# Streaming two tiles through two layers instead of one tile through both, in an eight-core hybrid decoder step

## The chip, the cores and the metric

The kernel runs on all eight NeuronCores of one Trainium2 chip. Each core has its own data and no core talks to another. The metric is the device time of one execution in microseconds (us), taken from the slowest core. The program has a second, slower state in which one die runs at a lower granted clock (in one run of the kernel before: 731.43 us, with 0.756 to 0.768 on cores 0 to 3 and 0.853 to 0.856 on the others); runs in that state are left out of every comparison.

Engines are named as in the profile: PE is TensorE's matmul, PEld its weight load, DVE is VectorE, ACT is ScalarE, POOL is GpSimd, SP is the queue that issues loads and stores. The program gives each engine one queue of instructions and orders the engines against each other by semaphores. A wait therefore also holds back what stands behind it in the same queue; the timelines below show this, GpSimd's above all (on ACT, in e8, a square that waited 11.15 us).

## The reference, cut to what matters

Per core there is one prompt sequence of 2048 tokens and 16 sample sequences of 4 tokens. Both go through two layers and a final norm:

```
def recurrent_layer(x, ...):                      # layer 0
    u = rmsnorm(x, g)
    xb, gate = split(u @ w_in)                    # 1024 -> 2 x 1024
    xc = causal_conv(xb)                          # 4 taps
    r, i = sigmoid(block-diagonal gates of xc)    # 8 blocks of 128
    a = exp(-8 r softplus(-lam));  h_t = a h_{t-1} + sqrt(1 - a^2) i xc
    return x + (h * silu(gate)) @ w_out

def pool_layer(x, ...):                           # layer 1
    u = rmsnorm(x, g)
    xb, gate = split(u @ w_in)
    z = ((windowed mean of xb over 2, 4, 8, 16) - xb) @ w_grp ...
    return x + (z * silu(gate)) @ w_out
y = rmsnorm(pool_layer(recurrent_layer(x)), final_norm)
```

The recurrence, the convolution and the pooling carry state from one tile of 512 tokens to the next, so the four prompt tiles of a layer must stay in order. Layer 1 of a tile and layer 0 of the next tile are independent of each other.

## The kernel before

A helper records each operation with what it reads and writes, derives the semaphore waits, and emits one in-order queue per engine. A layer of a tile is cut into four steps of two 128-channel chunks. The parts:

```
# The norm of one 128-token row group s of a tile; XS and the PSUM banks PS0/PS1 exist twice, UT once.
def N2(tl, s, key):   # POOL: XS[s % 2] = X * rstd
    S.run("pool", tensor_scalar(out=xs, in0=X, scalar1=ssc, ...), reads=[bXB[b][s], bSS], writes=[bXS[s % 2]])
def N3(tl, s):        # PE: eight 128x128 transposes into bank s % 2
    S.run("pe", trf, reads=[bXS[s % 2], bIDB], writes=[bPS[tb]])
def N4(tl, s, grow):  # DVE: UT[:, :, rows of s] = bank * gain
    S.run("dve", tensor_tensor(out=UT[:, :, s*128:...], in0=tbv, in1=gbc, op=mult), reads=[bPS[tb], bVT], writes=[bUTs[s]])

def inproj(l, tl, m, psi):   # PE: eight matmuls over all four row groups of UT
    S.run("pe", f, reads=bUTs + [bW_in[l][widx]], writes=[bPS[psi]])

def A1evac(l, tl, j):        # per chunk: the halo on POOL, the chunk on DVE (layer 0) or ACT (layer 1)
    S.run("pool", tensor_copy(out=ext[:, 0:HL], in_=Hh[:, c, :]), writes=[bEXT[ci]])
    S.run("dve" or "act", copy(out=ext[:, HL:HL+Tt], in_=PS[2 + 2*ci]), writes=[bEXT[ci]])
    S.run("pool", tensor_copy(out=Hh[:, c, :], in_=ext[:, Tt:Tt+HL]), reads=[bEXT[ci]])
# ... E0b: multiply, scan and gate on DVE, and on POOL a copy of the scan's last column into HSTp

def layer0(tl, next_tl):
    ...
    for j in range(4):
        if j + 1 <= 3: A1evac(0, tl, j + 1)
        if j == 3:     out_part1(0, tl)
        E0a(tl, j)
        if j + 1 <= 3: A1silu(0, tl, j + 1); CASTRI(tl, j + 1)
        E0b(tl, j)
        if j + 1 <= 3: TANHV(tl, j + 1)
        if j + 2 <= 3: A1pe(0, tl, j + 2)      # the projection runs one step ahead
# then out_part2 per row group, residual add, square, N2, N3, N4, and layer1 of the same tile
```

Inside a layer the input projection of step j+2 is queued at the end of step j, so PE runs a step ahead. At the end of a layer everything drains: output projection, residual add, norm, and only then the next layer's first projection.

## Time and profile before

The median is 705.5 us (five runs, 703.8 to 706.41).

| what | us | from |
|---|---|---|
| first projection of the first tile | 31.15 | timeline of PE |
| one tile in the steady state, two layers and two seams | 147.2 | timeline of PE |
| sample projection starts | 623.97 | timeline of PE |
| end of the span | 702.3 | page |
| PE, DVE, ACT, POOL busy | 488, 457, 343, 144 | page |
| granted clock, mean | 0.85 to 0.86 | cores |

Two groups of the kernel before, from the page's list of costliest instructions. The columns are line, engine, operation, names and shapes, count, busy us and mean ns, then the idle time before them and the releaser of most of it:

```profile
L494 PE MATMUL PS<-UT,W_in 128*128 128x512 bf16 x1024 | 264.0, 423 | 10.5 <-DVE UT L472 10.5
...
L462 PE MATMUL PS<-IDENTB,XSreg 128*128 128x128 bf16 (+1 forms) x272 | 22.0, 228 | 34.0 <-POOL XSreg L450 14.0
```

The first is the input projection; PE hardly waits for its operand (10.5 us in all). The second are the transposes of the norms. PE was idle 34.0 us before them, of which 14.0 us ended with GpSimd's scaled row.

### The profile page before, as it was taken

How to read it: one execution, taken by the hardware profiler on the slowest of the kernel's cores; microseconds unless marked ns; L12 is line 12 of the kernel's file. 1: busy time of each engine (PE TensorE's matmuls, PEld its weight loads, DVE VectorE, ACT ScalarE, POOL GpSimd, SP SyncE). 2: the span in 40 equal slices, each digit the busy share in tenths (PEclk: the TensorE clock that was granted, in tenths of full speed). 3: DMA queues.
4: the chain of work that ended last, by engine and by line, in shares of the span. 5: the costliest groups of instructions: out<-in, count | busy, mean ns of one | idle time of the engine just before them, and what ended most of it. 6: DMA issues, size and time to landing. Idle time of an engine off the chain costs nothing.

```text
span 702.3 us, 8514 instructions; the slowest of 8 cores (700.1 to 702.3 us)
## 1 busy us (share of the span) xinstructions
PE 487.8 (69%) x2352; PEld 216.9 (31%) x2352; DVE 456.8 (65%) x670; ACT 343.4 (49%) x554; POOL 144.0 (21%) x270
## 2 busy tenths in 40 slices
PE   0476576898766687976766679786566889761645
PEld 0232223443322233433222234333222334341332
DVE  0668877583668866856588767746788668457262
ACT  1368863243078753533488735531778626324211
POOL 4213312120301113323011132412021223121000
PEclk9998978799998778999888789999876989996766
DMA  9999980300000000050000000420000001203003
GB/s 217 157 163 166 162 129 12 121 1 0 1 1 0 1 0 1 31 179 31 0 1 0 0 1 1 151 91 0 0 1 0 1 0 43 93 2 119 16 11 67
DMA packets 19845, 34.65 MB, mean 49 GB/s; under 512 B 3539, under 2 KB 12755, under 8 KB 19798
## 3 DMA queue, kind: packets, MB, share of 16 engines
q0 software_dynamic: 13552, 13.63, 13.8%
q1 hardware_dynamic: 6246, 20.46, 9.6%
q8 instruction: 20, 0.33, 0.2%
q14 instruction: 27, 0.22, 0.1%
HBM read 37.75 MB, written 9.97 MB: 68 GB/s over the span
## 4 chain that ended last, share of the span: by engine, by line
PE 41%; DVE 29%; issue 12%; ACT 12%; POOL 3%; DMA 2%; DVEq 1%; ACTq 0%; POOLq 0%; SPq 0%
PE PS L494 20%; PE PS L515 10%; DVE TMP L620 8%; DVE EXT L593 3%; PE PS L532 3%; DVE UT L472 3%; DVE H L682 3%; ACT JUNK L419 3%; DVE TMP L616 3%; DMA XSreg<-vecs 2%; PE PS L755 2%; DVE TMP L679 2%; ACT A2M L764 2%; PE PS L893 1%; POOL XSreg L450 1%
## 5 line engine op out<-in xcount | busy, mean ns | idle before, releaser
L494 PE MATMUL PS<-UT,W_in 128*128 128x512 bf16 x1024 | 264.0, 423 | 10.5 <-DVE UT L472 10.5
L494 PEld LDWEIGHTS PS<-UT,W_in 128*128 128x128 bf16 x1024 | 109.8, 108 | 162.7 <-issue 67.6
L515 PE MATMUL PS<-W_out,HG 128*128 128x512 bf16 x288 | 73.5, 420 | 13.5 <-ACT TMP L608 9.0
L620 DVE SCALAR_TENSOR_TENSOR TMP<-EXT,VT,TMP 128x512 f32<-128x512 f32 x96 | 72.1, 751 | 10.7 <-DVE TMP L620 0.5
L638 PE MATMUL PS<-XCB,W_r 128*128 128x512 bf16 x32 | 15.8, 495 | 81.9 <-ACT XCB L628 43.4
L532 PE MATMUL PS<-W_out,HG 128*128 128x512 bf16 (+1 forms) x256 | 62.1, 403 | 9.7 <-DVE HG L773 9.1
L608 ACT ACTIVATE TMP<-PS 128x512 f32<-128x512 f32 x64 | 35.8, 598 | 60.5 <-PE PS L494 60.4
L538 DVE TENSOR_TENSOR XB<-PS,XB 128x512 f32<-128x512 f32 (+1 forms) x68 | 44.8, 687 | 29.8 <-PE PS L532 26.0
L596 ACT ACTIVATE EXT<-PS 128x512 f32<-128x512 f32 x32 | 19.1, 598 | 84.4 <-PE PS L494 55.1
L450 POOL TENSOR_SCALAR XSreg<-XB,SS 128x1024 bf16<-128x1024 f32 (+1 forms) x34 | 37.9, 1118 | 64.6 <-ACT SS L423 43.0
L515 PEld LDWEIGHTS PS<-W_out,HG 128*128 128x128 bf16 x288 | 30.0, 106 | 58.5 <-issue 32.3
L472 DVE TENSOR_TENSOR UT<-PS,VT 128x1024 bf16<-128x1024 bf16 (+1 forms) x34 | 39.3, 1187 | 10.3 <-PE PS L462 10.3
L462 PE MATMUL PS<-IDENTB,XSreg 128*128 128x128 bf16 (+1 forms) x272 | 22.0, 228 | 34.0 <-POOL XSreg L450 14.0
L773 DVE TENSOR_TENSOR HG<-A2M,TMP 128x512 bf16<-128x512 f32 x32 | 21.2, 688 | 37.6 <-ACT A2M L764 37.6
L695 POOL COPY HSTp<-H 128x1 f32<-128x1 f32 x32 | 22.2, 694 | 107.8 <-DVE H L682 107.8
L682 DVE TENSOR_TENSOR_SCAN H<-TR,HSTp,TMP 128x512 f32<-128x512 f32 x32 | 41.1, 1284 | 3.8 <-DVE TMP L679 1.0
L641 ACT ACTIVATE TR<-PS,DER 128x512 f32<-128x512 f32 x32 | 21.9, 685 | 38.0 <-DVE H L682 32.0
L532 PEld LDWEIGHTS PS<-W_out,HG 128*128 128x128 bf16 (+1 forms) x256 | 26.3, 105 | 45.3 <-issue 20.4
L764 ACT ACTIVATE A2M<-PS,DER,VT 128x512 f32<-128x512 f32 x32 | 23.1, 776 | 35.0 <-PE PS L755 35.0
L593 DVE COPY EXT<-PS 128x512 f32<-128x512 f32 x32 | 22.0, 687 | 27.9 <-PE PS L494 27.9
L729 DVE TENSOR_TENSOR TMP<-TMP 128x512 f32<-128x512 f32 (+3 forms) x48 | 33.5, 697 | 5.4 <-DVE TMP L729 0.5
L419 ACT ACTIVATE JUNK<-XB 128x1024 uint8<-128x1024 f32 (+1 forms) x21 | 21.9, 1045 | 27.8 <-DVE XB L538 27.6
(142 smaller groups left out, 640.8 us busy)
## 6 DMA issues: line engine op xcount, KB each, us to landing
y_p<-XB SPq DMA_DIRECT2D x16, 512.0 KB, 3.5
XB<-x_p SPq DMA_DIRECT2D x12, 512.0 KB, 4.8
W_in<-a_w_in POOLq DMA_DIRECT2D x4, 1024.0 KB, 28.3
W_in<-b_w_in POOLq DMA_DIRECT2D x4, 1024.0 KB, 20.9
XB<-x_p SPq DMA_DIRECT2D x1, 2048.0 KB, 11.6
W_out<-a_w_out POOLq DMA_DIRECT2D x2, 1024.0 KB, 49.1
W_out<-b_w_out POOLq DMA_DIRECT2D x2, 1024.0 KB, 23.4
XB<-st_pool SPq DMA_DIRECT2D x15, 64.0 KB, 5.6
```

Of the source, the lines that this page charges most:

```text
L419: S.run("act", lambda e: e.activation(out=junk, in_=X, func=AF.Square, accum_out=ssc), reads=[bXB[b][s]], writes=[bJUNK, bSS])
L450: S.run(N2_ENG, lambda e: e.tensor_scalar(out=xs, in0=X, scalar1=ssc, scalar2=0.0, op0=ALU.mult, op1=ALU.add), reads=[bXB[b][s], bSS], wri ...
L472: S.run("dve", lambda e: e.tensor_tensor(out=UT[:, :, s * 128:s * 128 + np_], in0=tbv, in1=gbc, op=ALU.mult), reads=[bPS[tb], bVT], writes ...
L494: last = e.matmul(PS[psi][:, 0:Tt], lhsT=W_in[l][:, k, m * 128:(m + 1) * 128], rhs=UT[:, k, 0:Tt], start=(k == 0), stop=(k == NCH - 1))
L515: last = e.matmul(PS[psi][0:np_, :], lhsT=HG[:, k, s * 128:s * 128 + np_], rhs=W_out[l][:, k, half * 512:(half + 1) * 512], start=(i_ == 0 ...
L532: last = e.matmul(PS[psi][0:np_, :], lhsT=HG[:, k, s * 128:s * 128 + np_], rhs=W_out[l][:, k, half * 512:(half + 1) * 512], start=(i_ == 0 ...
L538: S.run("dve", lambda e, Xh=Xh, psi=psi: e.tensor_tensor(out=Xh, in0=PS[psi][0:np_, :], in1=Xh, op=ALU.add), reads=[bPS[psi], bXB[b][s]], ...
L593: S.run("dve", lambda e, ext=ext, ci=ci: e.tensor_copy(out=ext[:, HL:HL + Tt], in_=PS[2 + 2 * ci][:, 0:Tt]), reads=[bPS[2 + 2 * ci]], writ ...
L608: S.run("act", lambda e, q=q, ci=ci: e.activation(out=SG[q][:, 0:Tt], in_=PS[3 + 2 * ci][:, 0:Tt], func=AF.Silu), reads=[bPS[3 + 2 * ci]], ...
L620: S.run("dve", lambda e, k=k: e.scalar_tensor_tensor(out=xc, in0=ext[:, k * St:k * St + Tt], scalar=vcol(c, V_CW0 + k), in1=xc, op0=ALU.mu ...
L682: S.run("dve", lambda e, h=h, a=a, bt=bt, c=c: e.tensor_tensor_scan(out=h, data0=a, data1=bt, initial=HST[:, c, 0:1], op0=ALU.mult, op1=AL ...
L764: S.run("act", lambda e, mi=mi, c=c, zt=zt: e.activation(out=zt, in_=PS[6 + mi][:, 0:Tt], func=AF.Identity, scale=vcol(c, V_BSCALE), bias= ...
```

## The change

The intent is to fill the seams. The four tiles no longer go through both layers one by one. Eight stages (layer 0 of tiles 0 and 1, layer 1 of tiles 0 and 1, the same for tiles 2 and 3) form one stream of 32 steps. Two neighbouring stages are independent, so the output projection of a stage is issued in eight groups inside the following stage, and the norm of the stage to come is placed in the third step (p == 2) of the stage before it. HG, the operand of the output projection, is doubled for this; the pool state lies in the second copy and is loaded at the end. UT, the operand of the input projection, still exists once. The core of the diff:

```diff
-        HG = sb("HG", [128, NCH, T], BF16)
+        HGt = [sb("HG0", [128, NCH, T], BF16), sb("HG1", [128, NCH, T], BF16)]
...
-        PTW = [TMP[:, 2048 + i * EXTW:2048 + (i + 1) * EXTW] for i in range(2)]
+        PTW = [TMP[:, 3072:3072 + EXTW], XSreg[:, 0:EXTW]]
...
+        stages = [(0, tiles[0]), (0, tiles[1]), (1, tiles[0]), (1, tiles[1]),
+                  (0, tiles[2]), (0, tiles[3]), (1, tiles[2]), (1, tiles[3])]
...
+            for i in range(nt):
+                X, p, j = tasks[i]
...
+                norm = p == 2 and ln is not None
+                soon = norm and (ln == 1 or X == 0)
+                late = norm and not soon
...
+                rows = carry + add_pend()            # residual adds of the stage before
+                if soon:
+                    N2r(tn, 0, (lk, 0))
+                    N2r(tn, 1, (lk, 1))
+                back_a(i)
+                if l == 1:
+                    issue(X - 1, nc_)                # output groups of the stage before
+                if soon:
+                    N3(tn, 0)
+                    N3(tn, 1)
...
+                back_b(i)                            # scans; HSTp copies on POOL
...
+                if soon:
+                    N4(tn, 0, gr)
+                    N4(tn, 1, gr)
+                    N2r(tn, 2, (lk, 2))
+                    N2r(tn, 3, (lk, 3))
...
+                if norm:
+                    N3(tn, 2)
+                    N3(tn, 3)
+                    N4(tn, 2, gr)
+                    N4(tn, 3, gr)
...
+                if n2 is not None:
+                    front1(n2)                       # input projection, a step ahead
+                    issue(X if p == 3 else X - 1, 2)
```

N2r is the reciprocal root (two small POOL operations) and N2. "Late" are the two handovers at which the next tile must first be loaded over rows that are still being stored: out of stage X3 (layer 1 of tile 1) and out of stage X4 (layer 0 of tile 2). I call the change from one stage to the next a handover; there are seven, numbered by the stage X0 to X6 that they end.

## The prediction

> **What bounds the kernel now.** I read four views in this order: the slices of the page, the table of windows cut at the edges of one tile (185.4 us, when the second tile's first layer-0 projection starts, to 332.6 us, when the third tile's does), the timeline of VectorE inside one layer-0 step, and the timeline of TensorE across a layer's end. First the page:
>
> ```profile
> PE   0476576898766687976766679786566889761645
> DVE  0668877583668866856588767746788668457262
> PEclk9998978799998778999888789999876989996766
> ```
>
> Neither row is full: PE dips where DVE is high and the other way round, four times, once per tile. So no engine bounds the whole; two different ones bound two kinds of stretch. The windows say which (columns: stretch, length, busy of PE, PEld, DVE, ACT, POOL, granted clock, DMA share, GB/s):
>
> ```profile
> 216.36:232.32 15.96, 10.44 (x37) 3.94 (x36) 13.34 (x19) 12.67 (x19) 2.72 (x7) 0.82 0.01 1
> 248.70:272.09 23.39, 18.80 (x97) 8.62 (x98) 16.46 (x20) 13.19 (x26) 6.04 (x7) 0.86 0.00 1
> 286.00:293.80 7.80, 7.80 (x38) 3.56 (x37) 6.37 (x9) 4.77 (x9) 2.25 (x5) 1.00 0.01 2
> 309.14:332.63 23.49, 17.42 (x100) 8.34 (x101) 12.17 (x16) 5.94 (x10) 5.77 (x7) 0.99 0.23 68
> ```
>
> Row one is one of the four steps (two 128-channel chunks) of layer 0: DVE is busy 13.3 of 16.0 us. Row three is one of the four steps of layer 1: PE is busy all of it. Rows two and four are the seams, output projection plus residual add plus norm, after layer 0 and after layer 1: 23.4 and 23.5 us in which the next layer may not start. One tile is 63.3 us of layer 0 (185.40 to 248.70), a seam, 37.1 us of layer 1, a seam: 147.2 us.
>
> How full is DVE really in a layer-0 step? Its timeline:
>
> ```profile
> 229.20 0.69 DVE L697 TENSOR_TENSOR HG<-H,TMP 128x512 bf16<-128x512 f32 x1
> 229.81 0.68 DVE L679 TENSOR_TENSOR TMP<-TMP,A2M 128x512 f32<-128x512 f32 x1
> 230.60 1.28 DVE L682 TENSOR_TENSOR_SCAN H<-TR,HSTp,TMP 128x512 f32<-128x512 f32 x1
> ...
> 235.30 0.69 DVE L593 COPY EXT<-PS 128x512 f32<-128x512 f32 x1 [1.21 <-PE PS L494]
> 236.77 2.48 DVE L620 SCALAR_TENSOR_TENSOR TMP<-EXT,VT,TMP 128x512 f32<-128x512 f32 x3
> ```
>
> Between dependent instructions lies about 0.1 us that is not called idle; the only bracketed wait in the step is 1.21 us for PE. So a layer-0 step is 16.0 - 1.2 = 14.8 us of DVE work that nothing but DVE can shorten. The seam on PE:
>
> ```profile
> 247.05 0.63 PE L639 MATMUL PS<-XCB,W_i 128*128 128x512 bf16 x1
> 248.79 10.33 PE L515 MATMUL PS<-W_out,HG 128*128 128x512 bf16 x36 [1.11 <-DVE HG L697]
> 259.27 6.20 PE L532 MATMUL PS<-W_out,HG 128*128 128x512 bf16 x28
> 265.31 0.61 PE L462 MATMUL PS<-IDENTB,XSreg 128*128 128x128 bf16 x8
> ...
> 272.09 13.21 PE L494 MATMUL PS<-UT,W_in 128*128 128x512 bf16 x48 [1.48 <-DVE UT L472]
> ```
>
> 16.5 us of projection during which DVE finishes early and waits, then 6.8 us of square, scale, transpose, scale, then the next projection. 36 matmuls in 10.33 us is 287 ns each, 28 in 6.20 us is 221 ns: the first run partly at the low clock.
>
> [...] in layer 0 a run of matmuls starts 427 ns apart after the 3 to 4 us gaps around the gate matmuls and ends at 216 ns. [...] this trace shows clock 1.00 with PE full from 286 to 294 us on its core[...]. [...] the residual add measures 688. [...] The change leaves the number of loads in a layer-0 step at two.
>
> **The change part by part.** No arithmetic is taken away. Eight stages (layer 0 of tiles 0 and 1, layer 1 of tiles 0 and 1, the same for 2 and 3) make 32 steps in one stream. Two neighbouring stages are always independent, so the output projection of a stage (8 groups of 8 matmuls, over two PSUM banks), its residual adds, and the norm of the next but one are put among the steps of the following stage. HG is doubled for it, by laying the pool state over its second copy; so the pool state is loaded and transposed at the end instead of near the start.
>
> *Taken off:* the seams, 23.4 + 23.5 us a tile.
>
> *Put into a layer-0 stage*, on DVE, which bounds it: 8 adds at about 0.70 us spacing (7 took 4.87) = 5.6; 4 scalings into UT at about 1.15 = 4.6. Per stage: 4 x 14.8 = 59.2 + 10.2 = 69.4. At the third step all four UT pieces must be written before the next stage's projection may start, and DVE then waits for the first 8 of its matmuls, at 216 to 427 ns, 1.7 to 3.4 us, with the semaphores about 4. Total 73. A stage followed by layer 1 has no convolution in its last step: two scans with their multiplies 5.4 plus the widest pool 7.7, not 14.8, and PE is the next to wait on: 72. The stage after tile 1's layer 1 also gets 4 final scalings at 1.22 (4.9): 79. The first one has the small state transposes: 73. PE has room: its 16 gate, 128 input and 64 output matmuls and 32 transposes are 208 x 0.22 + 2.4 = 48 us at full clock, and filling its gaps should keep that clock.
>
> *A layer-1 stage* is bound by PE: (128 + 16 + 64) x 0.22 + 4 x 0.61 = 48 us. DVE has about 40: 20 tree adds and 8 subtractions over both chunks (19.5), 8 gates (5.5), 5.6, 4.6, up to 4.9. The norm chain (last add, square 1.25, rstd 0.5 to 1.4, scale 1.12, transpose 0.61, scaling 1.2, some 6 to 7 us) is entered in the third step with no projection left to cover it, so I add 5 to 6: 54, and 57 where the next is layer 0. The last stage has fewer projections and no next norm: 45.
>
> *Sum.* Start of the first projection 31 (measured 31.15), its first step 14.5 (45.73), stages 73 + 72 + 54 + 57 + 79 + 72 + 54 + 45 = 506, the last projection with the pool state's transposes mixed in 12: 564. In the old trace the sample tile's input projection begins at 623.97, and the rest to 702.3 is 78.3 us that the change reorders but hardly shortens. 564 + 78.3 = 642, plus the 3 us by which the time exceeds the span: **645 us**. Of the four tiles' 8 seams (188 us) I thus expect about 60 back; the other 128 us are the same matmuls, adds and scalings, put where DVE or PE is already the bound, and the new bubbles.
>
> **The rivals.**
> 1. *Full overlap.* Waits that I added as bubbles are covered (DVE's 4 us, PE's 5 to 6): stages of 69 and 49, about 38 us less, near 607; half of it 625. For it: PE's 4 us gaps and its cold start are just what is filled. Against: UT exists once, so each stage's first projection still hangs on four scalings.
> 2. *In-order stalls.* PE executes in order; an output group waits for DVE's add to free one of two banks, and the gate matmuls that feed ScalarE stand behind it. If each of the 16 layer-0 steps loses 2 us by that, +32: 677. Against: each add stands in DVE's order before the next group is needed.
> 3. *The clock falls.* [...] The trace before has dense stretches of 40 us without it.
> 4. *Loads at the start.* Tile 1's 2 MB is wanted by 78 us, while the weights fill the DMA engines to about 100 us (slices 1 to 6); ScalarE could stand 5 to 15 us in front of a square. Loading the pool state later gives 1 MB back.
>
> **Range and chances.** Rivals 2 and 4 in part and rival 1 in part give 622 to 670. Between 691 and 720 needs two rivals in full, or a stall that I don't see: 0.05; slower than 720: 0.02; faster than 691: 0.93.
>
> **What would show each step.** Right: the sample projection starts near 564 us; DVE over 85% busy in layer-0 stages; no stretch of 16 us with output matmuls alone; a recorded mean of the input projection's matmuls clearly below the old 423 ns, since the clock stays up; DVE's wait of about 4 us once per stage at the evacuation. DVE's total busy time near the old 457 us and PE's below 488, because only its cold share shrinks. Wrong: long waits of PE on bank-freeing adds (rival 2)[...], squares that wait for tile 1's load (rival 4), or a tail longer than 78 us. The prediction as a whole is wrong if the streamed stages are no shorter than 147 us a tile.

Where the recorded text is marked as cut, it gave rules and figures of the hardware that no trace or run of this case shows. No term of the sum went with them: it still reads 564 + 78.3 + 3, about 645 us. What is gone from rival 3 is its bill for a lower clock, which stood above the range of 622 to 670 us. The trace of the kernel before shows:

- After PE's wait of 2.10 us at 214.75 us (only two gate matmuls lie between) the projection starts with weight loads 427 ns apart and the granted clock is 0.50 from 215.55 to 218.95 us; from 220.65 us it is 1.00. Dense weight loads at 1.00 are 216 ns apart (253.78 to 258.63 us). This is what "cold" and "restart" mean below. That filled gaps keep the clock up was an expectation, which e3 tests; what "about 4" adds for semaphores is an estimate too (brackets of 0.17 and 0.23 us stand in the traces here).
- From 280 to 320 us PE is busy 34.1 of 40 us at a granted clock of 1.00: the "dense stretches" of rival 3.
- The mean residual add is 688 ns. The "loads in a layer-0 step" are ScalarE's table loads, 1283 ns each, for instance at 217.35 and 224.48 us.

## The result, and the profile after

The changed kernel takes 696.0 us (median of 9 runs, 695.13 to 700.07) against 705.3 us. A ratio is the mean time of one kernel's runs over that of the other's of the same rounds, so it isn't quite the ratio of the medians: here 0.988, with a 95 % interval of 0.986 to 0.989. The gain is real but within 2 %. The outputs are correct.

The page's slices of the kernel after (40 equal slices of the span, busy tenths; PEclk is the granted clock in tenths):

```profile
PE   0485666688389859936797167873898699761645
DVE  0657776888857655754688758898656567667262
PEclk9986766899689979976899659995999799985766
```

The dips of PE have not gone. They have become shorter and deeper: in the middle of the span single slices fall to 3, 3, 1 and 3, where the kernel before has none below 5, with drops of the granted clock (to 7, 6 or 5) next to them. The mean clock is 0.83 to 0.84, lower than before.

The windows of four stages after, cut at the first input projection of each stage (stretch, length, busy us of PE, PEld, DVE, ACT, POOL with counts, granted clock, DMA share, GB/s):

```profile
112.55:191.10 78.55, 56.66 (x240) 24.17 (x241) 64.49 (x84) 48.90 (x72) 19.65 (x38) 0.83 0.00 1
191.10:251.88 60.78, 49.00 (x236) 22.72 (x237) 40.37 (x68) 25.40 (x40) 15.45 (x30) 0.92 0.00 1
251.88:320.76 68.88, 51.16 (x240) 23.82 (x241) 39.68 (x52) 22.97 (x40) 19.25 (x36) 0.85 0.19 62
320.76:408.35 87.59, 58.05 (x244) 24.70 (x245) 64.28 (x84) 59.54 (x89) 21.54 (x42) 0.79 0.15 49
```

Stage X1 (layer 0) keeps DVE busy 64.5 of 78.6 us, stage X2 (layer 1) keeps PE busy 49.0 of 60.8. In both some 12 to 14 us belong to no bounding engine. X3 and X4, the late handovers, are worse. X1 to X4 carry two tiles in 295.8 us (112.55 to 408.35), 147.9 us a tile. The tile took 147.2 before. **The steady state has gained nothing**; the 8.6 us (sample projection at 615.42 instead of 623.97) come from the two ends of the stream.

The same two groups of the page as before, now after:

```profile
L502 PE MATMUL PS<-UT,W_in 128*128 128x512 bf16 x1024 | 256.4, 414 | 18.4 <-DVE UT L480 12.4
...
L470 PE MATMUL PS<-IDENTB,XSreg 128*128 128x128 bf16 (+1 forms) x272 | 30.4, 284 | 76.6 <-POOL XSreg L458 38.8
```

The projection's mean has gone from 423 to 414 ns only. PE's idle time before transposes has gone from 34.0 to 76.6 us, and the part released by GpSimd's rows from 14.0 to 38.8.

Here is one early handover, out of stage X1, on three engines. First PE's timeline (start, length, engine, line, operation, count, in brackets the idle time before it and the releaser):

```profile
176.24 0.61 PE L470 MATMUL PS<-IDENTB,XSreg 128*128 128x128 bf16 x8 [2.44 <-POOL SS L905]
177.99 1.01 PE L470 MATMUL PS<-IDENTB,XSreg 128*128 128x128 bf16 x8 [1.15 <-POOL XSreg L458]
...
181.91 0.63 PE L647 MATMUL PS<-XCB,W_i 128*128 128x512 bf16 x1
185.61 1.01 PE L470 MATMUL PS<-IDENTB,XSreg 128*128 128x128 bf16 x8 [3.07 <-POOL XSreg L458]
188.51 1.01 PE L470 MATMUL PS<-IDENTB,XSreg 128*128 128x128 bf16 x8 [1.88 <-POOL EXT L598]
191.10 9.24 PE L502 MATMUL PS<-UT,W_in 128*128 128x512 bf16 x34 [1.58 <-DVE UT L480]
```

Between 182.5 and 191.1 us PE does two us of transposes. It waits for GpSimd's rows, and then restarts on a low clock: 34 matmuls in 9.24 us are 272 ns each, at a granted clock of 0.50 from 191.10 to 194.50 us and 0.97 from there to 197.00. (The bracket at 188.51 names the halo copy of L598, because that ended last before it. By the code the transpose reads only the row, which ended at 188.26, 0.25 us before it, as at 185.61.) GpSimd in the same stretch:

```profile
182.33 0.71 POOL L707 COPY HSTp<-H 128x1 f32<-128x1 f32 x1 [2.08 <-DVE H L694]
183.12 0.19 POOL L903 TENSOR_SCALAR SS<-SS 128x1 f32<-128x1 f32 x1
183.46 0.55 POOL L905 TENSOR_TENSOR SS<-SS,NEGH 128x1 f32<-128x1 f32 x1
184.24 1.12 POOL L458 TENSOR_SCALAR XSreg<-XB,SS 128x1024 bf16<-128x1024 f32 x1 [0.23 <-POOL SS L905]
...
187.14 1.12 POOL L458 TENSOR_SCALAR XSreg<-XB,SS 128x1024 bf16<-128x1024 f32 x1 [0.23 <-POOL SS L905]
188.20 0.20 POOL L598 COPY EXT<-H1p 128x15 f32<-128x15 f32 x1
```

It copies the scan's last column (HSTp) only once DVE's scan has run; rows 2 and 3 stand behind that copy, and the halo copy of the next step stands behind the rows. DVE:

```profile
186.74 1.22 DVE L480 TENSOR_TENSOR UT<-PS,VT 128x1024 bf16<-128x1024 bf16 x1 [0.23 <-PE PS L470]
189.63 1.23 DVE L480 TENSOR_TENSOR UT<-PS,VT 128x1024 bf16<-128x1024 bf16 x1 [1.67 <-PE PS L470]
195.59 0.71 DVE L742 TENSOR_TENSOR TMP<-EXT 128x526 f32<-128x526 f32 x1 [4.74 <-ACT EXT L604]
```

DVE scales the last two row groups as they come, then has nothing until the projection's first output has been evacuated: 4.74 us. A late handover, out of stage X3, again on PE:

```profile
308.14 1.01 PE L470 MATMUL PS<-IDENTB,XSreg 128*128 128x128 bf16 x8 [9.13 <-POOL XSreg L458]
...
318.17 1.01 PE L470 MATMUL PS<-IDENTB,XSreg 128*128 128x128 bf16 x8 [4.08 <-POOL EXT L598]
```

The first transpose waits 9.13 us for its row and the last one 4.08 us more (for the row before the copy that the bracket names, as above). Here the reload takes part: ScalarE's squares at 309.18 and 314.18 us had waited 3.75 and 3.85 us for the load of tile 2.

### The profile page after: what moved, and what is told of

It is laid out like the page before. It is cut to its first block, busy times and chain, and to the rows that moved or that the text cites. A ratio compares the mean times of both kernels' runs of the same rounds, so it can differ in the third digit from the quotient of the medians.

```text
span 694.0 us, 8450 instructions; the slowest of 8 cores (690.7 to 694.0 us)
## 1 busy us (share of the span) xinstructions
PE 473.6 (68%) x2352; PEld 219.2 (32%) x2352; DVE 460.7 (66%) x670; ACT 336.4 (48%) x522; POOL 167.8 (24%) x320
## 4 chain that ended last, share of the span: by engine, by line
PE 43%; DVE 23%; issue 12%; ACT 12%; POOL 6%; DMA 3%; DVEq 1%; POOLq 0%; ACTq 0%; SPq 0%
PE PS L502 23%; PE PS L876 10%; DVE TMP L628 4%; DVE H L694 4%; POOL XSreg L458 3%; DVE TMP L691 2%; PE PS L943 2%; DVE UT L480 2%; DMA XSreg<-vecs 2%; DVE EXT L601 2%; POOL SS L905 2%; PE PS L540 2%; PE PS L768 1%; DVE TMP L624 1%; PE PS L470 1%
## 5 line engine op out<-in xcount | busy, mean ns | idle before, releaser
L502 PE MATMUL PS<-UT,W_in 128*128 128x512 bf16 x1024 | 256.4, 414 | 18.4 <-DVE UT L480 12.4
L502 PEld LDWEIGHTS PS<-UT,W_in 128*128 128x128 bf16 x1024 | 107.0, 105 | 164.1 <-issue 64.1
L876 PE MATMUL PS<-W_out,HG 128*128 128x512 bf16 x448 | 103.6, 383 | 4.2 <-DVE XB L885 4.2
L470 PE MATMUL PS<-IDENTB,XSreg 128*128 128x128 bf16 (+1 forms) x272 | 30.4, 284 | 76.6 <-POOL XSreg L458 38.8
L628 DVE SCALAR_TENSOR_TENSOR TMP<-EXT,VT,TMP 128x512 f32<-128x512 f32 x96 | 74.3, 774 | 10.7 <-DVE TMP L628 0.5
L885 DVE TENSOR_TENSOR XB<-PS,XB 128x512 f32<-128x512 f32 x64 | 43.9, 688 | 43.2 <-PE PS L876 38.7
L876 PEld LDWEIGHTS PS<-W_out,HG 128*128 128x128 bf16 x448 | 44.0, 98 | 58.3 <-issue 6.3
L777 ACT ACTIVATE A2M<-PS,DER,VT 128x512 f32<-128x512 f32 x32 | 23.1, 773 | 69.8 <-PE PS L768 69.8
L480 DVE TENSOR_TENSOR UT<-PS,VT 128x1024 bf16<-128x1024 bf16 (+1 forms) x34 | 39.8, 1188 | 24.5 <-PE PS L470 24.4
L895 ACT ACTIVATE JUNK<-XB 128x1024 uint8<-128x1024 f32 (+1 forms) x41 | 43.5, 1060 | 22.9 <-DVE XB L885 14.0
L470 PEld LDWEIGHTS PS<-IDENTB,XSreg 128*128 128x128 bf16 (+1 forms) x272 | 23.6, 128 | 87.5 <-issue 87.0
L607 POOL COPY H0p<-EXT 128x3 f32<-128x3 f32 x32 | 6.0, 188 | 137.5 <-DVE EXT L601 137.5
L616 ACT ACT_TABLE_LOAD x17 | 21.8, 1283 | 34.0 <-PE PS L502 33.8
L742 DVE TENSOR_TENSOR TMP<-EXT 128x526 f32<-128x526 f32 (+3 forms) x32 | 23.1, 721 | 18.5 <-ACT EXT L604 18.5
```

The lines of the kernel that those rows point to most:

```text
L470: last = e.transpose(out=tbv[:, k, :], in_=xs[:, k * 128:(k + 1) * 128], identity=IDENTB[0:np_, 0:np_])
L480: S.run("dve", lambda e: e.tensor_tensor(out=UT[:, :, s * 128:s * 128 + np_], in0=tbv, in1=gbc, op=ALU.mult), reads=[bPS[tb], bVT], writes ...
L502: last = e.matmul(PS[psi][:, 0:Tt], lhsT=W_in[l][:, k, m * 128:(m + 1) * 128], rhs=UT[:, k, 0:Tt], start=(k == 0), stop=(k == NCH - 1))
L616: S.run("act", lambda e, q=q, ci=ci: e.activation(out=SG[q][:, 0:Tt], in_=PS[3 + 2 * ci][:, 0:Tt], func=AF.Silu), reads=[bPS[3 + 2 * ci]], ...
L628: S.run("dve", lambda e, k=k: e.scalar_tensor_tensor(out=xc, in0=ext[:, k * St:k * St + Tt], scalar=vcol(c, V_CW0 + k), in1=xc, op0=ALU.mu ...
L742: S.run("dve", lambda e, dst=dst, src=src, lo=lo, hi=hi, sh=sh: e.tensor_tensor(out=dst[:, lo:hi], in0=src[:, lo:hi], in1=src[:, lo - sh:h ...
```

## The experiments

Each kernel is the changed kernel with one edit unless it says otherwise. "Wrong on purpose" means that the outputs are wrong and only the time counts. Times are medians; the kernel before, in the same rounds, took 704.6 to 706.3 us. Stage lengths are read from PE's timeline at the first input projection of each stage. The edits are shown shortened. Because the kernel before moved by 1.7 us between rounds, a difference of 2 us or less between runs of different rounds is not read as an effect.

My first theory was that the handovers cost more than I had allowed, by a serial chain of rows over GpSimd (A) or by the cold restart of TensorE (B). The rivals were the reload of tiles 2 and 3 (C), and rival 2 or 3 of the prediction, a cost inside the plain steps.

### 1. Rows early, no GpSimd in the chain, a warm array, no reload

`e1_rows_early` (correct): at the five early handovers rows 2 and 3 go ahead of the HSTp copies, and the four scalings between the two chunks of the step.

```diff
-                    front2b(n1) ... back_b(i); N4(0); N4(1); N2r(2); N2r(3) ... N3(2); N3(3); N4(2); N4(3)
+                    front2b(n1); N2r(2); N2r(3); E0b(tl, j, only=0)
+                    N4(0); N4(1); N3(2); N3(3); N4(2); N4(3); E0b(tl, j, only=1)
```

> The changed kernel with one reordering, results unchanged: at the five handovers whose next tile is already in place (into stages 2, 3, 4, 7 and 8 less the two that wait for a reload, so stages 0 to 1, 1 to 2, 2 to 3, 5 to 6, 6 to 7) the scale-and-cast of rows 2 and 3 is put on GpSimd before the state copies that it stood behind, and the four scalings into UT are put between the two chunks of the step instead of after both. Same instructions, same counts. Theory A (each handover is a serial chain square, rstd, scale, transpose, scaling that runs after the step's own work is used up): 3 to 6 us off each of the five, 15 to 28 us off in all, 696 to about 668 to 681, and TensorE's idle time before the norm transposes falls by a similar amount. Theory B (the stream is held by throughput or by the lower clock): within 5 us of 696.

Measured: 683.54 us, ratio 0.968 [0.967, 0.970]. 12.5 us came off, less than theory A wanted. The edit moves rows, transposes and scalings together, so it doesn't say which of the moves paid.

`e2_no_pool_in_chain` (wrong): the transposes read a constant, so TensorE doesn't wait for GpSimd, which still does all its row work.

```diff
-  S.run("pe", trf, reads=[bXS[s % 2], bIDB], ...)      # in_=xs
+  S.run("pe", trf, reads=[bW_r, bIDB], ...)            # in_=W_r
```

> Wrong results on purpose: in the stream the norm transposes read a constant weight tile instead of the scaled rows, so every instruction stays and only the link from GpSimd's scaling to TensorE's transpose is cut, at all seven handovers. Theory A (norm chain): TensorE no longer waits for GpSimd before transposes (54 us of waits on that in the changed kernel), the handover shrinks to transpose, scaling, projection; 25 to 45 us off, 651 to 671 us. Theory B (throughput or clock): 690 or more.

Measured: 682.48 us (2 runs), ratio 0.966 [0.964, 0.969]: -13.5 us. Taking GpSimd out of the chain altogether is worth hardly more than the reordering.

`e3_warm` (correct): six dummy 128x512 matmuls ahead of each handover transpose.

```diff
+                    warm(s)      # 6 matmuls of resident weights into bank s % 2
                     N3(tn, s)
```

> Results unchanged: six useless 128x512 matmuls into the bank of each norm transpose, just before it, at all seven handovers, so that TensorE is not idle while it waits and the next projection need not start at half rate. Theory B (cold restarts are what the handover costs): first projection matmuls after a handover at about 216 instead of 427 ns, 1.7 us or more off each of seven, 684 us or less. Theory A: the chain is what counts and the dummies may lie in its way; between 690 and 710.

Measured: 683.73 us, ratio 0.969 [0.967, 0.972], granted clock 0.88 to 0.89. PE's timeline of this run at the late handover out of X3 (L912 are the dummies):

```profile
309.99 1.46 PE L912 MATMUL PS<-W_in 128*128 128x512 bf16 x6
311.60 0.61 PE L470 MATMUL PS<-IDENTB,XSreg 128*128 128x128 bf16 x8
313.79 7.07 PE L502 MATMUL PS<-UT,W_in 128*128 128x512 bf16 x32 [1.58 <-DVE UT L480]
```

The 32 matmuls of the projection now take 7.07 us, 221 ns each, where the changed kernel took 8.83. From the start of a stage's first input matmul to that of its sixteenth the changed kernel takes 4.7 to 5.6 us at the seven handovers; here it is 3.23 us at five of them and 4.92 at two (into X2 and X7). So the cold restart is a cost too (B).

`e4_no_reload` (wrong): tiles 2 and 3 are not loaded.

```diff
-                final_piece_b(tl, s, next_user[id(tl)])
+                final_piece_b(tl, s, None)       # for tiles 2 and 3
```

> Wrong results on purpose: tiles 2 and 3 are not loaded over the finished tiles 0 and 1 (eight loads of 512 KB less), all compute is the same. Theory C (the two handovers into stages 4 and 5, which exceed my estimate by 12 us each, wait for store, then load, in one in-order queue): 8 to 20 us off, all of it before those two handovers, 676 to 688. If the norm chain alone makes them long: 4 us or less off.

Measured: 692.79 us (2 runs), ratio 0.981: -3.2 us. The reload (C) is a small part.

### 2. Do the two repairs add up, does the clock matter before, what is the upper bound?

`e5_rows_warm` (correct): both edits, e1 and e3.

> Both repairs at once: rows 2 and 3 normalised early on GpSimd, and six dummy matmuls ahead of each handover transpose. Alone they gave -12.5 us (683.5) and -12.3 us (683.7) against the changed kernel's 696. If the serial norm chain and the cold restart of TensorE are two separate costs, the sum is about -24: 670 to 675 us. If both removed the same idle time (the dummies only fill a wait that the early rows also shorten), the two together give little more than one: 680 to 684.

Measured: 684.12 us, ratio 0.969 [0.968, 0.971], clock 0.88 to 0.89. No sum at all. By stages, the early handovers are not better than in e1 (X2 60.9 us against 59.0, X6 60.6 against 59.1), probably because the dummies now stand in a chain that hardly idles: into X3, PE works off the four groups of dummies and transposes back to back from 237.51 to 245.88 us. At the late ones X4 takes 85.4 us as in e3 (88.7 in e1), X3 66.4 (64.8 in e3, 67.4 in e1).

`e6_before_warm` (correct): the same dummies in the kernel before.

> The kernel before with the same six dummy matmuls ahead of each transpose of the prompt tiles, so at its seams and at its first norm. The control for the clock theory: if a cold restart after idle TensorE time is a property of any handover, this kernel also gains, 1.5 to 2 us at each of its seven seams, so 692 to 696 us instead of 706. If the gain of the dummies is particular to the changed kernel's order, it stays within 2 us of 706.

Measured: 723.27 us (3 runs), ratio 1.025 [1.023, 1.027]: 18 us slower, at a higher clock (0.87 to 0.88 against 0.85 to 0.86). My expectation was wrong. From the last output matmul of layer 0 to the next projection the same seam now lasts 9.7 us instead of 6.6 (272.9 to 282.60 against 265.5 to 272.09), while the warm projection shortens the layer-0 part of a tile from 63.4 to 62.0 us only, since DVE bounds it. A tile took 153.3 us instead of 147.2. **A higher granted clock is not a shorter time.** So the dummies paid only where they took the place of idle time (e3), not here, where they lengthened the seam by 3.1 us.

`e7_no_norm` (wrong): no square, row, transpose or scaling at any prompt handover; the next stage reads the stale operand.

```diff
-                    sq(tn, ...); N2r(tn, ...); N3(tn, ...); N4(tn, ...)
+                    pass
```

> Wrong on purpose: the changed kernel without any norm at the seven prompt handovers (no squares, no GpSimd rows, no transposes, no scalings; the next stage reads the stale operand). Upper bound on what the handovers cost. The plain steps took 16 to 17.8 us and the handover steps 27.5 to 33.4, so if the whole miss of the prediction sits in the handovers, taking them away gives about 10 to 11 us at five of them and 20 at the two late ones, some 90 us: 600 to 620 us, at a granted clock above 0.88. If the stages are held by something else (DVE work of the residual adds[...]), the time stays above 640 us.

Measured: 604.65 us (2 runs), ratio 0.857, clock 0.88. As expected. PE's timeline of this run at the handover out of X1:

```profile
164.97 0.63 PE L647 MATMUL PS<-XCB,W_i 128*128 128x512 bf16 x1
165.39 12.16 PE L502 MATMUL PS<-UT,W_in 128*128 128x512 bf16 x48
```

The next stage's projection follows the gate matmuls at once: PE is a step ahead again. **The seven handovers cost 696.0 - 604.65 = 91.4 us, 13 us each.** The plain steps hold their sizes: stages X1, X2, X5, X6 take 65.9, 48.9, 68.4 and 49.3 us.

`e8_late_early` (correct): e5, and the two late handovers reordered; the outgoing final norm at the start of a step, two stores ahead of two loads.

```diff
+                    fin = rows_sq(rows)              # squares ahead of the step's ACT work
+                    for ...: rs(...)
...
+                    finish(fin)                      # ahead of back_b; stores first, then loads
```

> The combined kernel of the first run, and in addition the two late handovers (layer 1 to layer 0 of tile 2, layer 0 to layer 0 of tile 3) reordered: the final norm of the outgoing rows is computed at the start of a step instead of its end, the two stores go ahead of the two loads, and rows 0 and 1 of the incoming tile are normalised before the step's last scans. The two stages lasted 68.9 and 87.6 us against 60.8 and 78 at the early handovers, so up to 8 to 9 us each could come off: 656 to 668 us. If the late handover is held by the transfers themselves (the store, then the load into the same rows), 0 to 4 us come off: 668 to 673.

Measured: 699.52 us, ratio 0.991: 15 us worse than e5. X3 gained (62.6 us against 66.4) and X4 went from 85.4 to 109.2 us. ACT's timeline in X4 shows why:

```profile
335.08 1.06 ACT L897 ACTIVATE JUNK<-XB 128x1024 uint8<-128x1024 f32 x1 [11.15 <-DVE XB L887]
```

The square stands in front of ACT's exponentials and waits 11.15 us for a residual add that DVE has yet to do; DVE in turn needs the exponentials. Three more squares of this stage wait 2.29, 7.96 and 2.29 us in the same way, 23.7 us with the first. In e5 such waits in X4 are 6.3 us in all, so they make up most of what X4 lost. An early place in an in-order queue is only early if its input is.

### 3. Splitting the 91 us

`e9_scalings_only` (wrong): e7, but the four scalings on DVE stay at their places and read a constant of the same shape.

```diff
+                    N4(tn, s, gr)        # in0=W_r, out=UT, where the change has it
```

> Wrong on purpose: of the handover norms only the four scalings on VectorE are kept (they read a constant of the same shape), so squares, GpSimd rows and transposes are gone. Without any norm the time was 604.65 us, with all of it 696. The prediction charged the scalings with their whole length: 28 x 1.15 to 1.23 us = 32 to 34 us, hence 632 to 640. If VectorE hides them in its waits, the time is 605 to 615.

Measured: 667.01 us (2 runs), ratio 0.946: +62.4 us over e7, for 28 scalings that keep DVE busy for 33 us. That is above both expectations. PE at the handover out of X1:

```profile
173.15 0.63 PE L651 MATMUL PS<-XCB,W_i 128*128 128x512 bf16 x1
180.74 11.99 PE L506 MATMUL PS<-UT,W_in 128*128 128x512 bf16 x48 [6.96 <-DVE UT L484]
```

and DVE at the same place:

```profile
178.14 2.35 DVE L484 TENSOR_TENSOR UT<-W_r,VT 128x1024 bf16<-128x1024 bf16 x2
185.02 0.71 DVE L746 TENSOR_TENSOR TMP<-EXT 128x526 f32<-128x526 f32 x1 [4.53 <-ACT EXT L608]
```

The scalings stand behind the scans and the gate multiplies in DVE's order. The next projection waits for them (6.96 us here; 6.9, 7.0, 9.8, 13.6, 7.0, 6.9 and 8.9 at the seven handovers, 60 us in all), and then DVE waits for the projection: 4.53 us. The lead of one step that PE had in e7 is lost at each handover.

`e10_no_rows` (wrong): transposes of a constant and scalings; no squares, no rows.

> Wrong on purpose: transposes (of a constant) and scalings kept, squares, reciprocal roots and row scalings (ScalarE and GpSimd) gone. An earlier run kept the row work but took it out of the chain in front of TensorE, and took 682.5 us. If the cost is the shuttling between TensorE and VectorE over two PSUM banks in in-order queues, this run stays at 670 to 682. If it is the row work itself (squares on ScalarE, rows on GpSimd, in front of other work in their queues), this run falls to 640 to 655.

Measured: 666.83 us (2 runs), ratio 0.945. Transposes add nothing to the scalings. Together with e2 (682.48) this says that the row work costs 15.7 us even where TensorE doesn't wait for it, and another 13.5 us where it does.

`e11_late_l1` (correct): e1, dummies at the late handovers only, and the late handover out of layer 1 as in e8.

> Meant to be fast: the early rows at the five early handovers (683.5 us alone), the dummy matmuls only at the two late handovers, and the late handover out of layer 1 reordered as in the failed run, whose stage there took 62.6 us instead of 67.4. Adding the pieces of the stages: 683.5 - 4.8 - 3.3 (late handover out of layer 0: 85.4 instead of 88.7) = 675; range 672 to 678. If the dummies and the order hide each other again: 680 to 684.

Measured: 682.03 us, ratio 0.967 [0.966, 0.969]. X4 took 85.9 us (88.7 in e1), but X3 67.3, so the gain of e8 there did not come back.

`e12_late_both` (correct): e11, and rows 0 and 1 of the late handover out of X4 ahead of the scans.

> As the run before it, and the late handover out of layer 0 reordered too, differently from the failed run: finals stay where they were, but the squares and rows of the incoming rows 0 and 1 go ahead of the step's scans, and their transposes and scalings between the two chunks. The loads of rows 0 to 2 land 5 to 20 us before their use, so 4 to 8 us may come off: 667 to 672 us. If ScalarE stands in front of a load again, as in the failed run, it is slower than the run before it.

Measured: 685.79 us, ratio 0.972 [0.971, 0.974]: X4 went up from 85.9 to 89.6 us. It missed; I did not find out which queue holds it.

### 4. Work, coupling and position

`e13_scalings_uncoupled` (wrong): as e9, but the scalings write a scratch buffer that PE doesn't read.

```diff
-  S.run("dve", ..., out=UT[...], writes=[bUTs[s]])
+  S.run("dve", ..., out=XS[s % 2], writes=[bXS[s % 2]])
```

> Wrong on purpose: the four scalings per handover stay in VectorE's order, but write a scratch buffer that TensorE does not read, so the next input projection does not wait for them. Without norms 604.65 us, with the coupled scalings alone 667. If the scalings cost their own length on VectorE, 28 x 1.2 = 34 us: 636 to 642. If what costs is that the next projection can no longer run a step ahead of VectorE (its waits for the scaled operand were 7, 7, 9.8, 13.6, 7, 6.9 and 8.9 us, 60 in all), the uncoupled scalings come to 605 to 625.

Measured: 622.38 us (2 runs), ratio 0.882. The bare 33 us of DVE work cost 17.7 us; the rest hides. So 667.0 - 622.4 = 44.6 us of the scalings' cost is the coupling to the projection through the one UT. (A second UT would be the direct test; no run tests this.)

`e14_rows_only` (wrong): squares, reciprocal roots and row scalings stay; no transposes, no operand scalings.

> Wrong on purpose: squares, reciprocal roots and row scalings kept in their places, transposes and operand scalings gone. If the row work loads ScalarE and GpSimd enough to delay the steps by itself: 615 to 635 us. If it only costs as a link of the chain in front of the scalings: 604 to 610.

Measured: 641.03 us (2 runs), ratio 0.908: +36.4 us, above both expectations, and nobody reads these rows. GpSimd's timeline at the handover out of X1:

```profile
174.86 0.71 POOL L707 COPY HSTp<-H 128x1 f32<-128x1 f32 x1 [2.07 <-DVE H L694]
175.66 0.52 POOL L903 TENSOR_SCALAR SS<-SS 128x1 f32<-128x1 f32 x1
...
179.73 1.12 POOL L458 TENSOR_SCALAR XSreg<-XB,SS 128x1024 bf16<-128x1024 f32 x1 [0.17 <-POOL SS L905]
180.79 0.20 POOL L598 COPY EXT<-H1p 128x15 f32<-128x15 f32 x1
```

and DVE's next wait:

```profile
181.85 0.71 DVE L742 TENSOR_TENSOR TMP<-EXT 128x526 f32<-128x526 f32 x1 [4.96 <-ACT EXT L604]
```

The rows of the coming tile (from 175.66) stand in front of the halo copy (180.79) that the next step's evacuation needs; ACT waits for it, and DVE waits for ACT. In the table of waits of this run DVE stood 20.1 us for ACT's evacuations and 17.9 us for GpSimd's halo copies, 38.0 us in all; in e7 neither is among DVE's ten largest waits, so each is below 4.2 us there. These 38.0 us are one wait at each of the seven handovers: 3.5, 5.0, 4.5, 8.7, 5.7, 5.0 and 5.6 us. Each ends just after a halo copy that stands directly behind row 3 in GpSimd's queue. Their sum is near the 36.4 us that the run lost, so the row work costs by its place in an in-order queue. The squares on ScalarE came back in this run too. They take part as a link: in three of the seven (out of X2, X3 and X6) GpSimd had first waited 4.07, 1.98 and 4.81 us for one. No run parts them from the rows.

`e15_scalings_first` (wrong): e9 with the scalings moved to the start of the step, when the previous projection has read UT.

```diff
                 rows = carry + add_pend()
+                if norm:
+                    for r_ in range(4):
+                        N4(tn, r_, gr)
```

> Wrong on purpose: the coupled scalings alone (667 us where the change has them), moved to the start of the handover step, just after the previous projection has read the operand. If the position at the end of the step is what takes the projection's lead away: 635 to 645, the bare VectorE length. If the single operand buffer itself is the cost wherever the scalings stand: 655 to 667.

Measured: 642.55 us (2 runs), ratio 0.911. Position alone is worth 24.5 of the 44.6 us.

`e16_rows_step_ahead` (correct): e1 with rows 0 and 1 normalised at the end of the second step and scaled at the start of the third; dummies at the late handovers.

> A correct kernel: rows early as in the first run (683.5 us), but at the five early handovers rows 0 and 1 are normalised at the end of the second step, transposed and scaled at the start of the third, and rows 2 and 3 follow behind the first scan; dummy matmuls only at the two late handovers. If position decides, some 3 us per early handover come off in addition to 3 for the dummies: 664 to 672 us. If the last scalings still stand behind the step's scans and decide alone, it is 680 to 684.

Measured: 689.37 us, ratio 0.977 [0.976, 0.979], worse than e1. By stages: X2 and X6 gain (56.1 and 56.0 us against 59.0 and 59.1), X0 gains (76.5 against 78.0), X1 and X5 lose (83.6 and 80.7 against 75.0 and 74.9).

`e17_mixed` (correct): the step-ahead order only in X0, X2 and X6, e1's order in X1 and X5, dummies at the late handovers.

> A correct kernel from the parts that gained stage by stage: rows a step ahead only in the first stage and in the two layer-1 stages that hand over to layer 1 or layer 0 of an early tile (76.5, 56.1 and 56.0 us in the last run against 78.0, 59.0 and 59.1 with rows early), rows early in the two layer-0 stages that hand over to layer 1 (75.0 and 74.9 against 83.6 and 80.7), dummy matmuls at the two late handovers (86.6 against 88.7). Summed by stage: 683.5 - 1.5 - 2.9 - 3.1 - 2.1 - 1 = 673; range 670 to 677. If the stages are not independent (what one gives back the next waits for), 680 or more.

Measured: 677.35 us (6 runs, 674.7 to 680.47), ratio 0.961 [0.958, 0.964]. This is the fastest correct version, faster than both kernels. It lies just above the range that I gave; the stages were 75.7, 75.7, 57.4, 66.8, 87.3, 73.9, 55.9 and 71.9 us.

## Why the prediction was wrong

It said 645 us, 622 to 670. The run gave 696.0. The table sets its stages beside three runs. All lengths go from one stage's first input projection to the next one's; since that projection runs about a step ahead of DVE, the predicted lengths are shifted by that step to compare (the sum is unchanged within 0.5 us). The leads that this uses, 15, 13, 11, 12, 15, 13 and 11 us, are my estimates after the result, from the prediction's own steps, so a single stage is comparable to some 2 us.

| stage | predicted | after | no norm | scalings only |
|---|---|---|---|---|
| X0, layer 0 | 72.5 | 80.9 | 68.2 | 74.6 |
| X1, layer 0 | 74 | 78.6 | 65.9 | 74.3 |
| X2, layer 1 | 56 | 60.8 | 48.9 | 58.6 |
| X3, layer 1, late | 56 | 68.9 | 45.8 | 61.5 |
| X4, layer 0, late | 76 | 87.6 | 78.3 | 83.7 |
| X5, layer 0 | 74 | 76.9 | 68.4 | 75.1 |
| X6, layer 1 | 56 | 60.5 | 49.3 | 58.2 |
| X7 and the last projection | 68.5 | 69.6 | 69.3 | 69.6 |

**What was right.** The tail: 78.3 us predicted, 78.6 measured. The start: 31 and 31.69. The plain steps of layer 1: 48 us for PE, 48.9 and 49.3 without norms. The plain steps of layer 0: 59.2 + 5.6 = 64.8 us, 65.9 and 68.4. DVE's total (460.7, "near the old 457") and PE's (473.6, below 488). DVE's wait of about 4 us at the evacuation: 4.74. One reading in it was loose: the gaps of "3 to 4 us" around the gate matmuls are 2.1 to 3.0 us of idle time in the trace (215 to 247 us).

**The rivals.** Rival 2 named banks: PE waited once, 4.2 us, for a bank-freeing add, so it fell. Rival 3 (a falling clock) fell too: the four layer-1 stages were granted 0.92, 0.85, 0.92 and 0.95, and the lower ones are the ones with idle time. In X7, granted 0.95, PE is busy 65.4 of 69.6 us; the other seven cores are 64.9 to 65.4 us busy in the same window, at 0.95 to 0.97. Rival 4 fell: the only two squares that waited for a load (3.75 and 3.85 us) waited for tile 2, not for tile 1.

**Its own signs.** DVE was to be over 85 % busy in layer-0 stages; it was 82 % in X1 and 73 % in X4. The prediction called itself wrong as a whole if the streamed stages were no shorter than 147 us a tile; they took 147.9. The result lies in the band to which it gave 0.05, for "two rivals in full, or a stall that I don't see"; it was the second.

**The step that failed** is the size of a handover, "4 scalings into UT at about 1.15 = 4.6" with "DVE then waits for the first 8 of its matmuls ... about 4" in layer 0, and "so I add 5 to 6: 54, and 57 where the next is layer 0" in layer 1. Four times 8.6 and 6 + 9 + 6 make 55 us for seven handovers. They cost 91.4 us (e7). Read by stages ("after" less "no norm" in the table), the four of layer 0 cost 12.7, 12.7, 9.3 and 8.5, together 43 us against 34 predicted, and the three of layer 1 cost 11.9, 23.1 and 11.2, together 46 us against 21. So the term that failed most is the "5 to 6" of layer 1. The runs divide the whole so:

| part | us | runs |
|---|---|---|
| DVE's own scaling work | 17.7 | e13 - e7 |
| its coupling to the projection through one UT | 44.6 | e9 - e13 |
| transposes | 0 | e10 - e9 |
| row work (squares, roots, rows) that PE doesn't wait for | 15.7 | e2 - e10 |
| row work in front of PE | 13.5 | after - e2 |

The scalings with their coupling, 62.4 us, are near my 55: the prediction had named this mechanism ("each stage's first projection still hangs on four scalings"). That the sizes are so near is partly luck. By stages ("scalings only" less "no norm") they cost 27 us in layer 0, where I had charged 34, and 34 in layer 1, where I had charged 21 for the whole chain; and I had charged the work in full and the bubble small, where e13 shows the opposite.

**What was missing is the row work, 29 us.** In layer 0 the sum charges it nothing, and in layer 1 only as part of the 5 to 6 us. The prediction doesn't weigh GpSimd's queue at all; at 21 % busy in the page before it looks like slack. But it copies the scan's last column and the next step's halo in order, so a row in front of a halo copy delays DVE (e14, at all seven handovers) and a row behind a last-column copy delays PE (the timeline of X1 above; e2 gives 13.5 us for all waits of PE on rows). No rival named this: rival 2 had in-order stalls, but in PE's queue, and the others looked at overlap, the clock and the loads.

One thing in the diff could be suspected as well: the pooling trees now share XSreg with the rows (PTW). In the trace of the changed kernel no idle time of DVE before a tree ends with a row or a transpose, and none of GpSimd before a row with a tree.

There is a smaller effect in the same place. In the changed kernel the multiply of L691 at 176.70 us took 1.32 us beside a row scaling on GpSimd that ran from 176.36 to 177.48, against 0.69 us for the same multiply at 180.12, when no row ran. The means go the same way: L628, L691 and L749 (into TR) take 772, 721 and 734 ns in e14, which has rows, and 751, 684 and 693 ns in e7, which has none at the handovers. No run shows the mechanism. DVE's busy time is 426.1 us in e14 against 421.8 in e7, so this is some 4 us of DVE work and not the main part.

**The rest of the miss.** Without any norm the kernel takes 604.65 us, and my sum without its 55 us gives 590, so about 15 us are outside the norms. 11 of them lie in X4 (78.3 us against 76 - 8.6 = 67.4), the stage with the final norm, the stores and the reload. e4 excludes the loads as the main part (X4 took 87.0 us there, 87.6 with loads); which part of the final norm it is has not been tested. The two parts of the miss, 91.4 - 55 = 36 and 15, give the 51 us.

**The clock** did not fill up as I had expected ("the clock stays up"): after each of the seven handovers the projection starts slowly (4.7 to 5.6 us for sixteen matmuls, see e3). e3 shows that this costs up to 12 us. e5 and e6 show that it is no separate item: it is a part of the same idle time, and it can't be added to the row work.

**Why the steady state gained nothing.** The change took away 46.9 us of seam a tile. In X1 to X4 without norms two tiles take 238.8 us (99.54 to 338.37), 119.4 each; the prediction's sum without its norms gives 115. The output matmuls and adds thus went into the steps, roughly as predicted. The four handovers then put back (295.8 - 238.8) / 2 = 28.5 us a tile, and the total is where it was before.

What stays open: how the row costs split at the late handovers (e8, e11 and e12 moved them both ways), and why the step-ahead order loses in X1 and X5. The parts are not strictly additive either: rows alone (36.4) and scalings alone (62.4) sum to 98.8, not 91.4.

## What to carry to other kernels

When work is moved out of a drained seam into a running pipeline, follow it through every in-order queue that it enters, above all the short queue of a helper engine that looks idle: ask what stands behind it. A single-buffered operand whose last writer sits at the end of a busy engine's step costs the lead of the next engine once per handover (44.6 us over the seven here, e9 - e13); write it at the start of the step (worth 24.5 us in e15, with a constant in place of the rows; with real rows, in e16, the order gained in three stages and lost more in two), or buffer it twice, which was not tested here. Remove the whole suspect first (e7) to learn its size, then put parts back one by one; single repairs of a chain tell too little, since two of them can buy the same idle time.
